# Seven block products for 22 of the 30 query, key and value blocks of each mixer, in a phase of their own

## The chip, the cores and the metric

One core of one Trainium2 chip. The metric is the device time of one execution in microseconds (us); lower is better.

## What is computed

Two layers of an encoder on 512 tokens of 1024 channels, all in float32. A layer is a feed-forward half-step, a mixer and a second feed-forward half-step. The change is in the mixer, which reads (cut):

```
u = rmsnorm(h, mix_pre_g[l])
proj = u @ w_in[l]
qa, ka, va, qb, kb, vb, qc, kc, vc, gl = jnp.split(proj, split_at, axis=-1)
oa = neighbourhood_attention(qa, ka, va, na_rpb[l])             # 8 heads
ob = sliding_window_attention(rope(qb), rope(kb), vb, sink[l])  # 8 query, 2 key heads
oc = differential_attention(rope(qc), rope(kc), vc, lam, ...)   # 4 heads, two maps each
yb = einsum('bsnc,ncd->bsnd', stack([oa, ob, oc], axis=2), w_branch[l])
gates = sigmoid(gl.reshape(b, s, 3, 1024) + b_gate[l])
h = h + rmsnorm(sum(gates * yb, axis=2) @ w_out[l], mix_post_g[l])
```

`w_in` has 54 column blocks of 128: four each of QA, KA, VA, QB, QC, KC and VC, one each of KB and VB (30 in all), and 24 of the gates (GL).

## The kernel before

Activations are kept transposed: channels on the 128 partitions, 512 tokens along the row. To keep float32 precision every operand is split into a rounded high part and a low part, and a product of two blocks is three matmuls, high by high, high by low, low by high (`mm3`, lines 319 to 324). A **plain dense block** (`dense1`, line 341) is one column block of a weight matrix: 8 row blocks, so 24 matmuls of 512 columns. A block against `w_branch` (`combine`, line 1584) has 4 row blocks, so 12 matmuls. Weights stream in tiles of 512 KB; ScalarE (ACT) makes the high part and VectorE (DVE) the low part of four blocks at a time (`ensure`, lines 220 and 221).

The feed-forwards (`ffn`, line 587) already take their gate and up blocks another way for most of the pairs: the activations and the weights are cut into 2 by 2 quarters, and **seven products** of quarters replace the eight of a plain pair (groups `p1` to `p7`, lines 892 to 913; the matmuls stand on line 878). A group of two column blocks is 7 x 4 x 3 = 84 matmuls of 256 columns. Sums of weight quarters and their splits are made by DVE and ACT for each group (lines 712 to 764), and quarter sums of the activations once for each feed-forward (lines 694 to 708).

In the mixer (`mixer`, line 1434) all 30 query, key and value blocks and the 24 gate blocks are plain. The first three (QA, KA, VA of pair 0) are made in the handover from the feed-forward (`begin`, line 402). Query and key blocks are evicted, rotated for branches B and C (`rope`, line 1421: four copies between partitions and three DVE operations), split, and copied into stacks with the high part over the low part (`stacks`, line 1336); value blocks are turned by TensorE transposes (`turn`, line 1352). A head of branches A and B is `softmax_pv` (line 1375): scores into a PSUM bank, DVE adds the bias and finds the maximum (line 1388), ACT takes the exponential (1397), DVE divides by the sum (1404), TensorE transposes (1412), the result is split, and two matmuls for each key block make the output (1415, 1416). Branch C is `attn_c` (line 1522). A gate block is evicted by ACT as a tanh (line 1581) and kept on the chip; `combine` multiplies it with the branch block on DVE (line 1588), and POOL adds it to the sum (line 1592).

The order of the work is the string `ORDER` (line 68), which traces units such as `qa1` (a pair's query, key and value blocks), `aa1` (its attention), `ga3` (a gate) and `ya3` (a branch block) one after the other. A compile-time scheduler then places the instructions of each engine by that order as a priority: what stands later may run ahead when its inputs and buffers are there. The ends of the phases are ordered by hand (`ordered`, line 416). PSUM has eight banks: four for dense blocks (`mm`), three for scores, transposes and small things (`at`), one for the head's output (`o`). Weight fetches of the mixer are issued on ACT's queue, those of the groups and nearly all other transfers on SP's.

## Time and profile before

| | before |
|---|---|
| median of 3 runs | 2397.39 us (2397.25 to 2400.49) |
| the profiled execution's span | 2398.4 us |
| TensorE (PE) busy | 2371.4 us, 99% |
| VectorE (DVE) busy | 1791.3 us, 75% |
| ScalarE (ACT) busy | 1340.1 us, 56% |
| GpSimd (POOL) busy | 155.3 us, 6% |
| moved by DMA | 340.45 MB, mean 142 GB/s |

The profiled execution's own time is its span, 2398.4 us from the first to the last instruction, 1.0 us above the median of the runs. Matmuls overlap in the profile (each is shown for longer than the distance to the next), so their pace is read from the distance between starts, or from evictions a known number of matmuls apart. The first mixer lies from about 347 to 858 us, the second from about 1547 to 2066 us; the rest are feed-forwards.

### The profile page before, as it was taken

Reading aid. Unit: us, or ns where it says so; the run is one execution under the profiler, and the core shown is the slowest. Engines: PE = TensorE matmul, PEld = TensorE weight load, DVE = VectorE, ACT = ScalarE, POOL = GpSimd, SP = SyncE. Lnnn points to the kernel's source line nnn. Section 1 sums busy time; section 2 is a strip of 40 time slices with the busy share of each in tenths; the row PEclk is TensorE's granted clock in tenths of the full one; section 3 lists DMA queues with packets and bytes.
Section 4 is the critical chain, followed back from the end, with each engine's and each line's share of the span. In section 5 each row is a group of like instructions: output and inputs, shape, how many; then the busy total and the mean of one; then the engine's idle time right before and its main releaser. Section 6 shows DMA issues by size and latency. Waiting matters only on the chain. (4 is left out here: it accounts for less than half of the span.)

```text
span 2398.4 us, 37669 instructions
## 1 busy us (share of the span) xinstructions
PE 2371.4 (99%) x14266; PEld 2083.0 (87%) x14266; DVE 1791.3 (75%) x2986; ACT 1340.1 (56%) x2493; POOL 155.3 (6%) x166
## 2 busy tenths in 40 slices
PE   9999999999999999999999999999999999999998
PEld 8999887888787889998899998878877788899987
DVE  7887975858767477888878878767676764788796
ACT  6565655646555365655655555556555554556563
POOL 0111000000001100110001110000000011011100
PEclk9999999999999999999999999999999999999999
DMA  5566546434443334665525565364354433346642
GB/s 168 160 172 188 162 142 177 128 106 138 123 135 97 106 111 136 164 165 166 174 90 166 160 176 192 120 186 121 104 142 129 110 104 123 97 144 172 185 147 91
DMA packets 119189, 340.45 MB, mean 142 GB/s; under 512 B 15968, under 2 KB 22752, under 8 KB 118496
## 3 DMA queue, kind: packets, MB, share of 16 engines
q1 hardware_dynamic: 91344, 224.72, 30.3%
q10 hardware_dynamic: 22032, 79.78, 11.1%
q0 software_dynamic: 5632, 33.56, 6.9%
q8 instruction: 112, 1.84, 0.3%
q14 instruction: 69, 0.57, 0.1%
HBM read 285.03 MB, written 48.23 MB: 139 GB/s over the span
## 5 line engine op out<-in xcount | busy, mean ns | idle before, releaser
L322 PE MATMUL mm<-X,w 128*128 128x512 f32 (+1 forms) x1044 | 396.5, 380 | 3.9 <-ACT w L220 2.1
L323 PE MATMUL mm<-X,w 128*128 128x512 f32 (+1 forms) x1044 | 396.7, 380 | 0.7 <-DVE X L550 0.7
L324 PE MATMUL mm<-X,w 128*128 128x512 f32 (+1 forms) x1044 | 395.0, 379 | 0.0
L221 DVE TENSOR_TENSOR w<-wr,w 128x512 fp32r<-128x512 f32 x360 | 250.3, 700 | 163.0 <-ACT w L220 161.5
L220 ACT ACTIVATE w<-wr 128x512 fp32r<-128x512 f32 x360 | 223.5, 627 | 222.7 <-PE mm L324 177.3
L878 PE MATMUL mm<-ht,l 128*128 128x256 f32 x1120 | 310.9, 278 | 0.0
L878 PE MATMUL mm<-ht,h 128*128 128x256 f32 x1120 | 310.9, 278 | 0.0
L878 PE MATMUL mm<-lt,h 128*128 128x256 f32 x1120 | 310.5, 277 | 0.0
L322 PEld LDWEIGHTS mm<-X,w 128*128 128x128 f32 x1044 | 197.2, 189 | 36.6 <-ACT X L549 2.6
L323 PEld LDWEIGHTS mm<-X,w 128*128 128x128 f32 x1044 | 197.3, 189 | 32.5 <-DVE X L550 1.1
L324 PEld LDWEIGHTS mm<-X,w 128*128 128x128 f32 x1044 | 197.1, 189 | 32.0
L878 PEld LDWEIGHTS mm<-lt,h 128*128 128x128 f32 x1120 | 210.8, 188 | 0.0
L878 PEld LDWEIGHTS mm<-ht,l 128*128 128x128 f32 x1120 | 210.6, 188 | 0.0
L878 PEld LDWEIGHTS mm<-ht,h 128*128 128x128 f32 x1120 | 210.5, 188 | 0.0
L1119 PE MATMUL mm<-wh,f 128*128 128x512 f32 x640 | 200.2, 391 | 0.0
L878 PE MATMUL mm<-X,h 128*128 128x256 f32 x1120 | 198.8, 277 | 0.0
L878 PEld LDWEIGHTS mm<-X,h 128*128 128x128 f32 x1120 | 170.0, 188 | 0.3
L878 PE MATMUL mm<-X,l 128*128 128x256 f32 x560 | 154.8, 277 | 0.0
L1119 PEld LDWEIGHTS mm<-wh,f 128*128 128x128 f32 x640 | 120.2, 188 | 25.5
L734 DVE TENSOR_TENSOR l<-wr,h 128x1024 fp32r<-128x1024 f32 x70 | 85.7, 1224 | 66.3 <-PE mm L878 66.3
L1119 PE MATMUL mm<-wl,f 128*128 128x512 f32 x320 | 125.5, 392 | 0.0
L1592 POOL TENSOR_TENSOR gate<-gate,gate 128x512 f32<-128x512 f32 x32 | 49.8, 1562 | 1155.3 <-DVE gate L1588 1049.3
(372 smaller groups left out, 5424.9 us busy)
## 6 DMA issues: line engine op xcount, KB each, us to landing
wr<-in_wts_dram SPq DMA_DIRECT2D x223, 512.0 KB, 4.7
wr<-in_wts_dram ACTq DMA_DIRECT2D x152, 512.0 KB, 3.6
sum<-in_wts_dram POOLq DMA_DIRECT2D x64, 512.0 KB, 5.4
st<-hi SPq DMA_DIRECT2D x84, 128.0 KB, 2.3
st<-lo SPq DMA_DIRECT2D x84, 128.0 KB, 3.7
ap<-in_wts_dram SPq DMA_DIRECT2D x20, 512.0 KB, 6.4
a<-kept SPq DMA_DIRECT2D x32, 256.0 KB, 6.3
ap<-sum SPq DMA_DIRECT2D x16, 512.0 KB, 3.3
```

The lines of the kernel that those rows point to most:

```text
L220: A.activation(hi, raw, AF.Copy)
L221: V.tensor_tensor(out=lo, in0=raw, in1=f(hi), op=ALU.subtract)
L322: PE.matmul(acc, w[0], x[0], start=start, stop=False)
L323: PE.matmul(acc, w[0], x[1], start=False, stop=False)
L324: PE.matmul(acc, w[1], x[0], start=False, stop=stop)
L734: V.tensor_tensor(out=W[g]["l1"], in0=raws[g][0], in1=f(W[g]["h1"]), op=ALU.subtract)
L878: PE.matmul(acc, ws[i], xs[j], start=start and k == n == 0, stop=stop and k == HK - 1 and n == 2, skip_group_check=True,)
L1119: PE.matmul(acc, x[i], w[j], start=start and n == 0, stop=stop and n == 2, skip_group_check=True)
L1592: G.tensor_tensor(out=merged[m], in0=merged[m], in1=t, op=ALU.add)
```

## The change

A new phase `p` (`project`) stands between the first feed-forward and the mixer of each layer. It makes all 30 blocks: eight of them plain (`COVER`, three in the handover as before) and 22 in 11 seven-product groups (`GROUPS`), with the feed-forward's group code moved into a class `Seven`. The first feed-forward's handover therefore also makes raw copies of its result, as the second's did. Query and key blocks of A, QB and KB are evicted, rotated where needed, split and written to memory; so are the turned and split values; QC and KC are written raw. Pair 0 of branch A stays on the chip. The mixer keeps attention, gates and branch blocks; it loads stacks and values from memory, and rotates and splits QC and KC after loading them. The second half of a head (transposes and output) is traced behind the scores of the next head (`rest`, `follow`). Scores have two banks of their own (`mx`), dense blocks two instead of four. Branch A's division by the sum moves from DVE to ACT. Gates of B and C are written to memory and loaded back for `combine`, through two tiles (`gd`). The order is new. The diff, cut to its core:

```diff
+COVER = (QA, KA, VA, QA + 1, KA + 1, VA + 1, KB, VB)
+GROUPS = (
+    (QA + 2, KA + 2), (VA + 2, VA + 3), (QA + 3, KA + 3), (QB, QB + 1), (QB + 2, QB + 3), (QC, KC), (QC + 1, KC + 1),
+    (VC, VC + 1), (QC + 2, KC + 2), (QC + 3, KC + 3), (VC + 2, VC + 3),
+) + tuple((GL + 2 * i, GL + 2 * i + 1) for i in range(0))
...
-qa0 qa1 aa0 aa1 qa3 qa2 aa3 aa2 kb ga2 ga1 ga0 qb0 ga4 ga5 ga7 ya5 ga3
-ga6 ab0 qb1 ya1 ya2 ya6 ya7 ab1 qb3 qb2 ya3 ya0 ya4 ab3 ab2 qc1 qc0 gb4
-gb0 gb1 ac0 yb0 yb1 qc2 gb2 yb2 ac1 gb3 qc3 gb5 ac2 yb4 yb5 gb6 yb6 fc2
-gb7 ac3 yb3 gc0 fc1 yb7 fc0 fc3 gc1 gc2 yc0 yc1 gc3 yc3 gc4 yc4 gc5 yc2
-gc7 gc6 yc6 yc7 yc5
+qa0 qa1 aa0 ga0 ga1 qa2 aa1 ga2 qa3 aa2 ga3 ga4 kb qb0 aa3 ga5 qb1 ab0
+ga6 ga7 gb0 qb2 ab1 gb1 gb2 qb3 ab2 ya0 gb3 ya1 gb4 qc0 ab3 ya2 gb5 ya3
+qc1 ac0 gb6 ya4 gb7 qc2 fc0 ac1 ya5 gc0 ya6 fc1 qc3 ac2 gc1 ya7 gc2 fc2
+ac3 yb0 gc3 yb1 gc4 fc3 yb2 gc5 yb3 gc6 yb4 gc7 yb5 yb6 yb7 yc0 yc1 yc2
+yc3 yc4 yc5 yc6 yc7
...
-    ABUFS = {"f": {"t": 4, "x": 10}, "m": {"t": 5, "h": 4, "rr": 2, "tx": 5, "st": 16, "g": 10, "s": 2, "pt": 4}}
-    PBUFS = {"mm": 4, "at": 3, "o": 1}
+    ABUFS = {"f": {"t": 4, "x": 10}, "p": {"t": 16, "x": 10, "rr": 2}, "m": {"t": 5, "h": 4, "rr": 2, "tx": 5, "st": 14, "gd": 2, "g": 10, "s": 2, "pt": 4}}
+    PBUFS = {"mm": 2, "mx": 2, "at": 3, "o": 1}
...
+        def seed_banks(self, x):
+            self.seeds = [bank("at") for _ in range(2)]
+            for t in self.seeds:
+                PE.matmul(t, x[:, 0, 0, :P], x[:, 0, 0:2, :], start=True, stop=True)
+
...
+    def project(l, op, accs):
...
+        def store(kind, x):
+            d = dr.tile([P, T], F32, tag=kind, name=nm(kind), bufs=60)
+            nc.sync.dma_start(d, f(x))
+            return d
...
+            made[c] = store("part", hi), store("part", lo)
...
+                made[c] = v if c == VA else [store("part", t) for t in v]
+            else:
+                made[c] = [store("part", t) for t in parts(tp)]
...
+        def turned_by(c, x):
+            sh = big("t", name="sh")
+            for q in range(4):
+                o = q ^ 1
+                nc.sync.dma_start(sh[32 * q : 32 * q + 32], x[32 * o : 32 * o + 32])
+            slowly.extend(
+                (
+                    lambda: V.tensor_tensor(out=x, in0=x, in1=turning[0], op=ALU.mult),
+                    lambda: V.tensor_tensor(out=sh, in0=sh, in1=turning[1], op=ALU.mult),
+                    lambda: V.tensor_tensor(out=x, in0=x, in1=sh, op=ALU.add),
+                    lambda: stacked(c, x),
+                )
+            )
...
+        def ready(c, x):
+            if c < VA:
+                stacked(c, x)
+            elif QB <= c < VB:
+                turned_by(c, x)
+            elif c < QB or c == VB:
+                turned(c, x, 2)
+            elif c >= VC:
+                turned(c, x, 1)
+            else:
+                made[c] = store("raw", x)
+
...
+        rest = [dense1(w, l, COVER[3], X, tag="at")]
+        for c, acc in zip(COVER, list(accs) + rest):
+            out(c, acc)
+        for n, c in enumerate(COVER[4:]):
+            out(c, dense1(w, l, c, X, tag=("mm", "at")[n % 2]))
+        while later:
+            later.pop(0)()
...
+        S.seed_banks(op.hi[0])
...
+                S.add22(g)
+            S.p2(g)
+            first_half(g)
+            if more:
+                S.low12(g + 1)
+                S.sum4(g + 1)
+                if g + 2 < count:
+                    S.fetches(g + 2)
+                else:
+                    fetch(1, nc.sync)
+                S.p5(g)
+                S.high24(g + 1)
+            work(3)
+        S.p3(count - 1)
+        second_half(count - 1)
+        other(count - 1)
+        work(len(slowly))
...
+            if sink is None:
+                A.activation(ss[i], ss[i], AF.Copy, scale=l[:, i : i + 1])
+            else:
+                V.tensor_scalar(out=ss[i], in0=ss[i], scalar1=l[:, i : i + 1], scalar2=None, op0=ALU.mult)
+        def rest():
+            op = bank("o")
...
+        def ask(hd):
+            raw = raws[hd] = big("g", name="braw")
+            nc.sync.dma_start(raw, bass.AP(rpb.tensor, (l * 8 + hd) * 16 * RPBW, [[RPBW, 8], [1, 16], [1, 8 * RPBW]]))
...
+        def load(d, dt=F32, tag="tx"):
+            x = big(tag, dt, name="x")
...
+        def rope(c):
+            x = load(made[c])
+            sh = big("tx", name="sh")
+            for q in range(4):
+                o = q ^ 1
+                nc.sync.dma_start(sh[32 * q : 32 * q + 32], made[c][32 * o : 32 * o + 32])
...
+            for s in range(2):
+                own, pair_ = slice(64 * s, 64 * s + 64), []
+                for one, two in ((hi, lo), (lo, hi))[: 2 if both else 1]:
+                    st = big("st", F32R, name="st")
+                    nc.sync.dma_start(f(st)[0:64], one[own])
+                    nc.sync.dma_start(f(st)[64:128], two[own])
+                    pair_.append(st)
+                res.append((pair_ + [None])[:2])
...
+        def follow(rest):
+            settle()
+            pending.append(rest)
...
+        def qkv_a(p):
+            for s in range(2):
+                ask(2 * p + s)
+            return restacked(QA + p, False), restacked(KA + p, True), values(VA + p)
...
+                rest = softmax_pv(
...
+                follow(rest)
...
-                t = gate0[m // 4][:, m % 4, :] if n == 0 else big("g", name="gate")
+                t = gate0[m // 4][:, m % 4, :] if n == 0 else big("gd", name="gate")
                 A.activation(t, pg, AF.Tanh, scale=0.5, bias=col("b_gate", l, n * KD + m))
+                if n:
+                    d = dr.tile([P, T], F32, tag="gate", name=nm("gate"), bufs=4 * KD)
+                    nc.sync.dma_start(d, t)
+                    t = d
                 gate[n, m] = t
...
+                if n:
+                    t = load(t, tag="gd")
...
+        with open_phase("p"):
+            made = project(l, X, accs)
         with open_phase("m"):
-            X, accs = mixer(l, X, accs)
```

## Rows read from the trace of the kernel before

**Rows 1.** The page: span, and busy us of each engine with its share, x instructions.

```profile
span 2398.4 us, 37669 instructions
...
PE 2371.4 (99%) x14266; PEld 2083.0 (87%) x14266; DVE 1791.3 (75%) x2986; ACT 1340.1 (56%) x2493; POOL 155.3 (6%) x166
```

**Rows 2.** Busy time by stretch; (x) instructions; last three: granted clock, DMA share, GB/s.

```profile
131.41:217.31 85.90, 85.90 (x754) 85.90 (x753) 72.66 (x92) 50.16 (x84) 14.97 (x18) 1.00 0.62 164
334.00:347.00 13.00, 12.61 (x64) 10.37 (x63) 11.45 (x20) 7.78 (x19) 0.00 (x0) 1.00 0.23 80
347.00:707.00 360.00, 354.48 (x1820) 294.54 (x1819) 248.46 (x610) 197.89 (x464) 4.30 (x3) 1.00 0.48 133
707.00:780.00 73.00, 72.60 (x352) 57.67 (x351) 52.12 (x104) 41.66 (x80) 10.32 (x7) 1.00 0.36 108
870.00:905.00 35.00, 35.00 (x230) 32.24 (x231) 24.74 (x35) 21.35 (x36) 0.00 (x0) 1.00 0.21 67
1190.00:1210.00 20.00, 20.00 (x125) 17.96 (x126) 16.57 (x31) 13.81 (x34) 0.00 (x0) 1.00 0.23 79
```

**Rows 3.** TensorE's waits: who waited for whom, us in all, times, longest.

```profile
PE at L1412 <- DVE s L1404: 2.9, 4, 1.9
```

**Rows 4.** Line 917, seed copy, once per group; 131 to 218 us; ns min/median/max, starts.

```profile
L917 ACT ACTIVATE at<-mm x10: 360/367/368, 131.4 to 217.3; 128x256 f32<-128x256 f32 x10
```

**Rows 5.** Timeline of ACT, 484 to 512 us: start, us, gate evictions [idle before].

```profile
490.86 0.69 ACT L1581 ACTIVATE gate<-mm,colt 128x512 f32<-128x512 f32 x1 [1.10 <-PE mm L324]
...
496.30 0.69 ACT L1581 ACTIVATE gate<-mm,colt 128x512 f32<-128x512 f32 x1 [2.09 <-PE mm L324]
```

**Rows 6.** PE's weight loads, 131 to 217 us: busy us, mean ns.

```profile
L878 PEld LDWEIGHTS mm<-ht,h 128*128 128x128 f32 x143 | 26.9, 188 | 0.0
```

**Rows 7.** DVE, 131 to 217 us: the gating product of the feed-forward.

```profile
L946 DVE TENSOR_TENSOR a<-t,v 128x512 f32<-128x512 f32 x9 | 6.1, 682 | 0.0
```

**Rows 8.** DVE by line and form, 347 to 780 us: count, busy us, mean ns.

```profile
L221 DVE TENSOR_TENSOR w<-wr,w 128x512 fp32r<-128x512 f32 x113 | 79.6, 705 | 48.4 <-ACT w L220 48.2
...
L1404 DVE TENSOR_SCALAR s<-s,l 128x256 f32<-128x256 f32 x48 | 14.7, 349 | 0.4
L349 DVE TENSOR_TENSOR lo<-x,hi 128x512 fp32r<-128x512 f32 x21 | 14.4, 688 | 6.4 <-ACT hi L348 4.8 <-DMA st<-hi 1.2
L349 DVE TENSOR_TENSOR lo<-at,hi 128x512 fp32r<-128x512 f32 x20 | 13.6, 687 | 7.6 <-ACT hi L348 7.6
...
L1429 DVE TENSOR_TENSOR x<-mm,cosR 128x512 f32<-128x512 f32 x13 | 8.9, 686 | 1.7 <-DMA sw<-lo 1.0 <-ACT raw L1423 0.7
...
L1362 DVE TENSOR_TENSOR v<-at,v 128x256 fp32r<-128x256 f32 x10 | 4.2, 420 | 1.7 <-ACT v L1361 1.7
```

**Rows 9.** Timeline of ACT, 380 to 480 us: head outputs (L1418), gates (L1581).

```profile
408.34 0.60 ACT L1418 ACTIVATE ot<-o 64x512 f32<-64x512 f32 x1
...
456.03 0.70 ACT L1581 ACTIVATE gate<-mm,colt 128x512 f32<-128x512 f32 x1
...
477.79 0.60 ACT L1418 ACTIVATE ot<-o 64x512 f32<-64x512 f32 x1
```

**Rows 10.** DMA issues: queue, count, KB each, median us from issue to landing.

```profile
wr<-in_wts_dram ACTq DMA_DIRECT2D x152, 512.0 KB, 3.6
...
a<-kept SPq DMA_DIRECT2D x32, 256.0 KB, 6.3
...
mask<-in_tables_dram SPq DMA_DIRECT2D x2, 256.0 KB, 4.5
```

**Rows 11.** The gates' combination on DVE and POOL, whole span.

```profile
L1592 POOL TENSOR_TENSOR gate<-gate,gate 128x512 f32<-128x512 f32 x32 | 49.8, 1562 | 1155.3 <-DVE gate L1588 1049.3 <-DVE nm L1536 80.4 <-DVE lc L1544 25.5
...
L1588 DVE SCALAR_TENSOR_TENSOR gate<-gate,mm 128x512 f32<-128x512 f32 x48 | 32.9, 685 | 25.0 <-PE mm L324 24.4
```

More of the change, by code (lines that the diff above doesn't have):

```diff
@@ L916, in seed @@
[L916 to L932 removed]
+        S.seed_banks(X.hi[0])
@@ L1442, in mixer @@
+        return rest
+    def mixer(l, op, made):
+        w, X = "w_in", op.blocks
+        masks, raws, turning = {}, {}, []
         for c0, n in ((0, 512), (512, 256)):
@@ L1577, in gates @@
+            follow(rest)
+        gate, merged = {}, [None] * KD
+        gate0 = made["gates"]
+        while len(gate0) < 2:
+            gate0.append(sb.tile([P, 4, T], F32, tag="n", name=nm("gate"), bufs=BUFS["n"]))
+        for _, c in GROUPS:
+            for m in (c - 1 - GL, c - GL) if c > GL else ():
+                gate[0, m] = gate0[m // 4][:, m % 4, :]
         def gates(n, *ms):
@@ L1614, in do @@
             kind, i = u[:2], int(u[2:] or 0)
+            if kind == "fc" or kind[0] == "y":
+                if kind == "fc" and i >= len(oc) or kind[0] == "y" and (kind[1], 3) not in OT:
+                    settle()
             if kind == "qa":
-                if i == 0:
-                    held[u] = qkv_a(*first)
-                else:
-                    early = second if i == 1 else []
-                    late = [dense1(w, l, c + i, X) for c in (QA, KA, VA)[len(early) :]]
-                    held[u] = qkv_a(*early, *late)
+                held[u] = qkv_a(i)
             elif kind == "kb":
-                held["kb"] = qkv_b(KB), turn(plain(dense1(w, l, VB, X), False), 2)
+                tables_in()
+                held["kb"] = qkv_b(KB), values(VB)
             elif kind == "qb":
@@ L1642, in mixer @@
             do(u)
-        M = [split(merged[m], "st", 0.5) for m in range(KD)]
+        M = [split(merged[m], "st" if m < 7 else "gd", 0.5) for m in range(KD)]
         hN = [big("s", shape=(P, 2, 2, T), name="h") for _ in range(2)]
```

682 lines of the change are left out of this document (427 added, 255 removed).

## The prediction, made before the result was known

> **What bounds the kernel now.** I read the page first: TensorE is busy for 2371.4 of the 2398.4 us of the span, VectorE (DVE) for 75% of it [rows 1]. So a matmul taken away is worth its full time as long as nothing else becomes late, and an engine at 75% is the one to watch. Then the table of stages, for idle time by stage: TensorE has none at all in the seven-product groups of a feed-forward (131 to 217 us), and 5.9 us (433 less 354.48 and 72.60) in the mixer from 347 to 780 us; the granted clock is 1.00 in each of these, the 2.4 GHz level [rows 2]. Then TensorE's list of waits, for what ends that idle time: the largest entry is a transpose that waits 2.9 us in all for a scaled score block from DVE [rows 3]. What is to be seen: the mixer is bound by TensorE because dense blocks fill the waits inside the attention. The change takes 27 of those fillers out of the mixer.
>
> **The change, part by part.** The sum is made on the profiled execution (2398.4 us, 1.0 us above the median of the runs).
>
> *Seven products.* Ten groups of a feed-forward lie nine periods apart, from 131.41 to 217.31 us: 9.54 us for one group of 84 half-width matmuls [rows 2, 4]. A pair of plain blocks is 48 full-width matmuls; two gate evictions with nothing between them lie 5.44 us apart [rows 5], so a pair takes 10.88 us. One group saves 1.34 us; 11 groups in each of 2 layers save 29.5 us.
>
> A half-width matmul carries a weight load of its own, of 188 ns [rows 6], and the rows show that it is hidden: 9.54 us over 84 is 114 ns a matmul, half of the 227 ns of 5.44 us over 24. The Trainium skill (TensorE: Matmul & The Clock Gate, Back-to-back issue gap) gives a sustained spacing of about 81 ns at 128 columns and 131 ns at 512 for streams of load and matmul; a straight line between them puts 256 columns at 98 ns (an estimate from that page), by which a group would cost 8.2 us against 6.3 us for a pair, and the change would lose 42 us. The trace disagrees with both of its spacings here.
>
> *Seeds.* Two more full-width matmuls in each layer (`seed_banks`), 4 x 0.227 = 0.9 us, on the path.
>
> *DVE in the new phase.* A group of the feed-forward costs DVE 72.66 / 9 = 8.07 us; without the gating product of 0.68 us it is 7.4 us [rows 2, 7]. The new phase adds the blocks' own work: rotating a block is three operations of 0.69 us and its split one more (2.75 us; five blocks), splitting a Q or K block of branch A 0.69 us (four), two value blocks of A 0.84 us each, four of C 0.69 us each [rows 8]: 20.9 us over 11 groups, 1.9 us each. That makes 9.3 us of DVE work against 9.54 us of TensorE. The cover is only 0.2 us a group, and the highest DVE share of a stretch in which TensorE did not wait is 85% (72.66 of 85.9) [rows 2]. Bounds: nothing, or 9.3 / 0.85 = 10.9 us a group, 15 us a layer. I take 1 us a layer, near the lower end, because weights are prepared a whole group ahead and the rotations are dealt out three at a time. ScalarE (50.16 of 85.9 us there) has room.
>
> *Ahead of the groups.* The eight plain blocks of this phase have the cover of the feed-forward's 870 to 905 us, where TensorE never waits and DVE has 10 us free [rows 2]; their evictions add about 3 us of DVE work: nothing. The raw copies that the first feed-forward's handover now makes are made today by the second's, where TensorE is busy 20.00 of 20 us, as against 12.61 of 13 in the first's [rows 2]: nothing, and if ScalarE were late there, 0.4 us.
>
> *Attention with less cover.* From 347 to 780 us TensorE loses 27 blocks of 5.44 us (three of the 30 were in the handover): 433 - 147 = 286 us remain. DVE has 248.46 + 52.12 = 300.6 us there [rows 2]; off go 54 weight splits of 0.705 us, 13 block splits of 0.69, five rotations of 2.06, ten value splits of 0.42 and four of 0.69, and the scaling of branch A's 32 score blocks of 0.35 that goes to ScalarE: 75 us [rows 8]. So 225 us over 286, 79% after 69%. But the new order ends on five gates and 16 branch blocks behind the last head, which need little DVE: 5 x 5.44 + 16 x 2.73 (12 matmuls of 0.227) = 71 us of TensorE with 26 splits and 16 combinations, 29 us of DVE. Ahead of them stand 215 us of TensorE against 196 us of DVE, 91%. At the 85% above those 196 us last 231: 16 us longer than TensorE's work. Two things speak for less. The program's order is run ahead of where it can be: gates that stand behind branch A's last two pairs were evicted from 456.03 us on, before its last head left at 477.79 [rows 9]; 49 us of the tail (five gates, eight blocks of branch B) can be run ahead the same way. And heads now overlap, where branch A's leave one by one, seven steps in 69.45 us [rows 9]. Bounds per layer: 5.9 us gained (all idle time gone) to 16 us lost. I take 5 us lost: cover gets thinner in the same stage that already waits.
>
> *From one phase to the next.* Masks and bias tables are loaded into tiles that lie where the new phase's were; a mask lands 4.5 us after its issue [rows 10]. Behind it wait the first head's scores; the first gates (5.44 us each, weights ready) cover it. Bounds 0 to 5 us a layer; I take 0.5.
>
> *Gates through memory.* Gates of branches B and C are written out and come back into a ring of two tiles (`gd`), on SP's queue. Stores wait in that queue for the tanh, loads for POOL's addition, and the stack loads and bias loads behind them wait with them; those are asked for a pair ahead. At the end 11 branch blocks follow each other. One turn of a tile is the load, 0.69 us on DVE and 1.56 us on POOL [rows 11]. Nearest rows for the load: 3.6 us (weights, twice the size) and 6.3 us (a kept row of this size, in a burst) [rows 10]. That gives (3.6 + 2.25) / 2 = 2.9 us a block against 2.73, or 4.3 us: 2 to 17 us a layer for 11 blocks. I take 2, since only one load is asked for at a time there, as with the weights.
>
> *Banks and transfers.* A dense block now has two banks in place of four; one is needed again 5.44 us (2.73 for a branch block) after its last matmul, and its eviction takes 0.69 us [rows 5, 11]: nothing, as long as that engine is less than 2 us late. In each layer 46 blocks of 256 KB are stored, twelve MB in about 105 us, on SP's queue between the weight fetches; they wait for splits that stand a few us ahead of the next fetch, and the sums that fill this stretch's queues in a feed-forward (0.62 of the DMA engines) are absent [rows 2]: nothing, and up to 0.5 us a group if a fetch does get caught behind a store, which is within the bound given for DVE there. Later the same halves are loaded as are copied on the chip today, plus 16 values and 16 gates.
>
> *Sum.* -29.5 + 0.9 + 2 x (1 + 5 + 0.5 + 2) = -11.6 us on 2397.4: **2386 us**.
>
> **Rivals.**
> 1. *All of it hidden* (2369 us). The overlap of heads and the run-ahead cover everything: -29.5 + 0.9. With today's idle time gone too it would be 2357. For it: seven-product groups already run without a wait at 85% of DVE. Against it: 91% ahead of the tail.
> 2. *DVE paces the attention* (2408 us, slower). Place: from the first head to the last of branch C. Price: 16 us a layer in place of my 5, so 2386 + 22. It decides from the point at which the scheduler runs less than 11 us of the tail's blocks ahead. If DVE also paced the new phase (15 us a layer) it would be 2436. Against it: today's order does run ahead [rows 9].
> 3. *The gate ring paces the tail* (2416 us). Place: the 11 branch blocks at the end; price 17 us a layer in place of 2. It decides once a gate takes over 3.2 us to land (2 x 2.73 less 2.25). For it: 6.3 us for the kept rows; against it: those are eight at once.
> 4. *Seven products cost more, not less*: half-width matmuls held to their 188 ns weight load would make a group 15.8 us, 4.9 above a pair, 108 us slower (2505 us). The groups of [rows 4] exclude it where they are; the page named above would have it in kind.
>
> **How the numbers follow.** My forecast has a chance of 0.46, rival 1 0.19, rival 2 0.25, rival 3 0.09, rival 4 0.01. The forecast's own range is 2376 to 2397. A measurement of this kernel can tell about 0.2% from no change, 4.8 us: faster is below 2392.6, slower above 2402.2. Faster: nearly four fifths of my forecast (0.36) and rival 1, 0.55. Same: the upper end of the forecast and the mild parts of rivals 2 and 3, 0.15. Slower: the rest, 0.30. The range, 2363 to 2416, takes in rival 1 with half of today's idle time gone below, and rivals 2 and 3 at their prices above; what is left out is both at once, or the new phase paced by DVE.
>
> **What would show it.** Right: groups of 9.5 to 9.7 us in the new phase; TensorE idle there under 3 us a layer; in the mixer between 8 and 14 us idle with DVE at 78 to 85%, waits ended by DVE; combinations in the tail 2.8 to 3.0 us apart. Wrong: periods over 10 us with DVE full (DVE paces the new phase); a mixer idle of 25 us or more (rival 2); combinations over 4 us apart that wait for a load (rival 3); no idle time at all (rival 1). What would make me wrong without showing in these: a transfer on SP's queue that holds the stacks of the next pair back, seen as scores waiting for a DMA.

## The result: 2405.4 us, 0.24% slower; the range held, the sign did not

| | before | after |
|---|---|---|
| median, same chip | 2399.62 us (9 runs, 2394.58 to 2402.60) | 2405.37 us (9 runs, 2398.53 to 2408.37) |
| ratio, 95% interval | | 1.0024 [1.0013, 1.0035] |
| the profiled execution's span | 2398.4 us | 2403.6 us |

The page of the changed kernel, the lines that answer to [rows 1]: TensorE's busy time fell by 14.6 us, with 796 more matmuls, and the span grew by 5.2.

```profile
span 2403.6 us, 39852 instructions
...
PE 2356.8 (98%) x15062; PEld 2109.1 (88%) x15062; DVE 1891.1 (79%) x3048; ACT 1425.7 (59%) x2671; POOL 156.5 (7%) x166
```

Busy time is not the whole of it, since a matmul at the lower clock counts as busy. So I split both spans another way: each matmul at its usual spacing (227 ns for 512 columns, 113.5 for 256, the same in both kernels), TensorE's idle time in the mixers (counted from the new phase's start), and what the granted clock took away, which is (1 less the granted clock) times the time that TensorE was busy at it.

| us, both layers | before | after | difference | forecast |
|---|---|---|---|---|
| matmuls at their usual spacing | 2325.3 | 2296.2 | -29.1 | -28.6 |
| idle time in the mixers | 14.3 | 33.8 | +19.5 | +17 |
| lost to the lower clock there | 0 | 9.0 | +9.0 | no term |
| the rest | 58.8 | 64.6 | +5.8 | no term |
| span | 2398.4 | 2403.6 | +5.2 | -11.6 |

The first row is a count times fixed spacings, as the forecast's was, so it shows only that the count was right; the pace itself is read from the groups below. The idle time as a sum came near the forecast. What turned the sign is the two rows under it: the lower clock follows waits, and the rest is what this account does not place. The clock differs from run to run: of the nine runs of the changed kernel the fastest, 2398.53 us, has a mean granted clock of 0.997, the others 0.994 to 0.996. Here are the stages of the first mixer in the changed kernel, in the columns of [rows 2]: cover blocks, seven-product groups, the start of the attention, its middle, branch C, the tail.

```profile
335.30:398.00 62.70, 62.36 (x371) 54.98 (x369) 48.23 (x71) 39.18 (x78) 0.00 (x0) 1.00 0.45 140
398.00:508.00 110.00, 109.26 (x942) 108.12 (x941) 91.80 (x126) 70.41 (x132) 0.00 (x0) 1.00 0.61 201
508.00:560.00 52.00, 46.05 (x238) 38.06 (x237) 28.93 (x97) 34.77 (x95) 0.00 (x0) 0.97 0.81 208
560.00:700.00 140.00, 139.06 (x737) 116.14 (x736) 123.60 (x336) 102.76 (x263) 0.00 (x0) 1.00 0.59 173
700.00:760.00 60.00, 57.66 (x267) 45.61 (x266) 48.18 (x100) 32.69 (x67) 5.01 (x3) 0.97 0.72 209
760.00:860.00 100.00, 94.97 (x429) 75.41 (x429) 57.89 (x100) 45.59 (x86) 20.48 (x13) 1.00 0.48 150
...
530.00:533.00 3.00, 3.00 (x12) 2.51 (x12) 0.00 (x0) 0.00 (x0) 0.00 (x0) 0.56 0.86 252
...
718.00:721.00 3.00, 3.00 (x11) 2.41 (x10) 2.55 (x6) 1.15 (x3) 0.00 (x0) 0.52 0.07 25
...
1715.80:1718.50 2.70, 2.66 (x16) 2.37 (x17) 0.42 (x1) 0.45 (x3) 0.00 (x0) 1.00 0.69 208
...
1733.60:1736.00 2.40, 2.40 (x8) 1.91 (x8) 0.00 (x0) 0.00 (x0) 0.00 (x0) 0.50 0.69 202
...
1906.70:1909.00 2.30, 2.30 (x6) 1.82 (x7) 1.98 (x4) 0.60 (x1) 0.00 (x0) 0.50 0.04 13
```

Three of the six stages lose time, and not the one in the middle, where DVE is busy for 88%: start 5.95 us, branch C 2.3, tail 5.0 (in the second layer 7.8, 3.3 and 5.4). The short windows stand behind long waits. Behind four of them, of 3.80, 1.90, 4.65 and 2.88 us, TensorE comes back at 0.50 to 0.56, that is, at the 1.2 GHz level for all or most of the window, and is busy all the while, with few matmuls done (6 in 2.3 us at 1906.7). Behind four others the clock stays at 1.00: 2.69 us (the window from 1715.8), and 1.65, 1.67 and 2.04 us (at 546, 798 and 1989 us). So the length of a wait alone does not decide it here.

TensorE's list of waits in the changed kernel names the three causes (us in all, times, longest):

```profile
PE mx L1659 <- DMA st<-part: 12.8, 4, 4.7
PE mm L326 <- DVE x L1912: 8.2, 8, 2.0
PE o L1871 <- DVE lo L353: 4.8, 2, 2.9
```

**Start.** The scores of branch A's pair 1 wait for stacks. The timeline of SP's queue there, and in branch C (start, us, line, DMAs):

```profile
516.37 0.80 SPq L1762 DMA_DIRECT2D st<-part  x1
...
520.54 0.45 SPq L1762 DMA_DIRECT2D st<-part  x1
526.09 0.45 SPq L1763 DMA_DIRECT2D st<-part  x1
...
707.84 1.02 SPq L465 DMA_DIRECT2D gain<-in_rows_dram  x2
708.95 0.58 SPq L1739 DMA_DIRECT2D x<-raw  x1
...
712.22 1.79 SPq L465 DMA_DIRECT2D gain<-in_rows_dram  x2
```

Masks and bias tables go first, the first stack is asked for at 516.37 us, and the queue then stops for 5.5 us behind the issue at 520.54, and again later. The queue's own list of waits (505 to 545 us) says what ended the two long stops:

```profile
SPq L1763 <- DMA wr<-in_wts_dram: 11.0, 2, 5.9
```

That is no transfer of this queue, but a weight load, issued on ACT's queue (for the first stop at 516.77 us, landed at 526.07). The program gives its transfers eight semaphores in turn, over both queues; the stack's load takes over the weight load's, and is not issued before that has landed. No run here gives the two their own semaphores, so how much of the wait this makes is open. Over the start the DMA engines are busy for 0.81 at 208 GB/s.

**Branch C.** The handover's gain rows, 1 MB and not needed for another 140 us, are issued around a query block's loads. DVE's timeline shows what that does: the rotation (L1748) waits 2.91 us for its load, and the split that TensorE needs (L353) stands behind it on the same engine. The second fence has TensorE's rows, the first of them for the start, the second for branch C.

```profile
715.08 0.69 DVE L1748 TENSOR_TENSOR x<-x,cosR 128x512 f32<-128x512 f32 x1 [2.91 <-DMA x<-raw]
716.35 1.28 DVE L353 TENSOR_TENSOR lo<-at,hi 128x512 fp32r<-128x512 f32 x2
```

```profile
529.94 0.47 PE L1659 MATMUL mx<-st,st 128*128 128x256 f32 x2 [3.80 <-DMA st<-part]
...
717.09 0.50 PE L1871 MATMUL o<-lo,x 128*128 128x512 f32 x1 [1.90 <-DVE lo L353]
```

**Tail.** Combinations (L1912) come 3.74 us apart where a branch block takes 2.73. The timelines of DVE, POOL and ACT, interleaved by start here, show a closed loop from the second row on: combination, POOL's addition, the high part on ACT, the low part on DVE, and only then the next combination. DVE's queue holds the low part ahead of that combination. The tail's longest wait (1.67 us at 798 us, 2.04 in the second layer) is not of this loop: there the combination itself waits for a gate's load, as the first row shows. That load was issued at 793.68 us, when POOL's addition had just freed one of the two tiles.

```profile
797.44 0.69 DVE L1912 SCALAR_TENSOR_TENSOR x<-x,mm 128x512 f32<-128x512 f32 x1 [1.74 <-DMA x<-gate]
...
812.22 0.68 DVE L1912 SCALAR_TENSOR_TENSOR x<-x,mm 128x512 f32<-128x512 f32 x1
813.04 1.61 POOL L1916 TENSOR_TENSOR gate<-gate,x 128x512 f32<-128x512 f32 x1 [2.13 <-DVE x L1912]
814.68 0.63 ACT L355 ACTIVATE hi<-gate 128x512 fp32r<-128x512 f32 x1 [2.59 <-POOL gate L1916]
815.35 0.69 DVE L356 SCALAR_TENSOR_TENSOR lo<-gate,hi 128x512 fp32r<-128x512 f32 x1 [1.85 <-ACT hi L355]
815.96 0.68 DVE L1912 SCALAR_TENSOR_TENSOR x<-x,mm 128x512 f32<-128x512 f32 x1
```

**Groups.** The seed copies of the new phase, once per group, in the columns of [rows 4]: ten periods in 98.9 us, 9.89 us each (10.08 in the second layer).

```profile
L719 ACT ACTIVATE at<-mm x11: 363/369/392, 398.5 to 497.4; 128x256 f32<-128x256 f32 x11
```

### The profile page after: what moved, and what is told of

Same layout as the page of the kernel before. It is cut to its first block, busy times and chain, and to the rows that moved or that the text cites. A ratio compares the mean times of both kernels' runs of the same rounds, so it can differ in the third digit from the quotient of the medians.

```text
span 2403.6 us, 39852 instructions
## 1 busy us (share of the span) xinstructions
PE 2356.8 (98%) x15062; PEld 2109.1 (88%) x15062; DVE 1891.1 (79%) x3048; ACT 1425.7 (59%) x2671; POOL 156.5 (7%) x166
## 5 line engine op out<-in xcount | busy, mean ns | idle before, releaser
L326 PE MATMUL mm<-X,w 128*128 128x512 f32 (+1 forms) x602 | 229.6, 381 | 3.1 <-ACT X L553 1.8
L327 PE MATMUL mm<-X,w 128*128 128x512 f32 (+1 forms) x602 | 229.1, 380 | 0.8 <-DVE X L554 0.7
L328 PE MATMUL mm<-X,w 128*128 128x512 f32 (+1 forms) x602 | 229.6, 381 | 0.0
L680 PE MATMUL mm<-ht,l 128*128 128x256 f32 x736 | 205.8, 280 | 0.0
L680 PE MATMUL mm<-ht,h 128*128 128x256 f32 x736 | 205.6, 279 | 0.0
L680 PE MATMUL mm<-lt,h 128*128 128x256 f32 x736 | 204.9, 278 | 0.0
L680 PE MATMUL mx<-lt,h 128*128 128x256 f32 x736 | 203.6, 277 | 0.0
L680 PE MATMUL mx<-ht,h 128*128 128x256 f32 x736 | 203.5, 277 | 0.0
L680 PE MATMUL mx<-ht,l 128*128 128x256 f32 x736 | 203.4, 276 | 0.0
L680 PE MATMUL at<-X,w 128*128 128x256 f32 x1104 | 141.2, 277 | 0.0
L680 PEld LDWEIGHTS mx<-lt,h 128*128 128x128 f32 x736 | 138.3, 188 | 0.1
L680 PEld LDWEIGHTS mx<-ht,h 128*128 128x128 f32 x736 | 138.2, 188 | 0.1
```

Of the source, the lines that this page charges most:

```text
L326: PE.matmul(acc, w[0], x[0], start=start, stop=False)
L327: PE.matmul(acc, w[0], x[1], start=False, stop=False)
L328: PE.matmul(acc, w[1], x[0], start=False, stop=stop)
L680: PE.matmul(acc, ws[i], xs[j], start=start and k == m == 0, stop=stop and k == n - 1 and m == 2, skip_group_check=True,)
```

## The experiments

Each ratio is to the kernel before, run on the same chip. What an edit does to the changed kernel is the difference of its ratio from 1.0024, times 2400 us, good to some 4 us. Diffs are against the changed kernel unless the text says otherwise.

### Two of the three waits mended

**e2, the gain rows later.** Their loads are issued behind those of branch C's first gate.

```diff
-        H = Handover(
+        with tc.issue_after(behind[0].ins):
+            H = Handover(
```

> Edit: the four row loads of the handover's gains (L465) are issued behind the first gate load of branch C on SP's queue, no longer beside the load of the last key block of branch C. Theory (that key block lands late because 1 MB of gains is loaded beside it, VectorE's rotation waits 2.9 and 3.9 us for it, and TensorE's second matmul of a C output waits behind that): the stalls of 1.90 us at 717.1 and 2.88 us at 1906.6 us go, and the half clock behind them, so the time falls by 7 to 10 us (4.8 us of waiting and about 5 us of half clock). Rival (the block is late because of its own stacks and weights in that stretch, the gains make no difference): the stalls stay within 1 us of what they are and the time within 3 us.

Measured: 2396.99 us, 0.9990 [0.9980, 1.0001], 8 us better than the changed kernel. The list of waits and the windows around branch C of both layers:

```profile
PE mx L1659 <- DMA st<-part: 11.8, 3, 4.4
PE mm L326 <- DVE x L1914: 7.3, 9, 1.2
```

```profile
700.00:740.00 40.00, 38.42 (x178) 29.77 (x177) 29.95 (x62) 22.01 (x44) 1.79 (x1) 1.00 0.68 181
1890.00:1920.00 30.00, 29.42 (x141) 22.78 (x139) 23.96 (x49) 14.55 (x29) 0.00 (x0) 1.00 0.75 206
```

L1871 falls from 4.8 to 0.5 us and the clock stays at 1.00. The two waits showed 4.8 us of idle time and gave 8 back. That points to a wait that costs more than its length, but 4.8 lies within the 4 us to which the 8 is known.

**e3, each split of the tail behind the next combination.** It takes the loop apart and leaves the ring of two gates as it is, so it tells the loop from rival 3's gate loads.

```diff
-        M = [split(merged[m], "st" if m < 7 else "gd", 0.5) for m in range(KD)]
+        M = []
+        for m in range(KD):
+            with tc.issue_after(made_[2, min(m + 1, KD - 1)].ins):
+                M.append(split(merged[m], "st" if m < 7 else "gd", 0.5))
```

> Edit: in the tail VectorE's split of merged block m is queued behind combination m+1, not ahead of it; the ring of two gate tiles stays. Theory (a loop over four instructions: combination, POOL's addition, ScalarE's high part, VectorE's low part, and the next combination stands behind that low part in VectorE's queue): combinations come down from 3.74 to 2.7 to 3.0 us apart, TensorE's waits of 0.74 us for them go, and the time falls by 5 to 9 us in the two layers. Rival (the ring of two gate tiles sets the 3.74 us: load, combination, addition): they stay over 3.5 us apart and the time within 2 us.

Measured: 2400.61 us, 1.0002 [0.9990, 1.0014], 5 us better. DVE's timeline in the tail:

```profile
811.13 0.67 DVE L1913 SCALAR_TENSOR_TENSOR x<-x,mm 128x512 f32<-128x512 f32 x1
...
814.19 0.68 DVE L1913 SCALAR_TENSOR_TENSOR x<-x,mm 128x512 f32<-128x512 f32 x1
```

3.06 us apart in place of 3.74, and TensorE's waits of 0.74 us are gone. The loop was the cause of the 3.74. The ring of two gates has another part: the first wait of the tail stays (1.88 and 1.96 us), and in this run too the combination ahead of it waits for a gate's load (1.95 us at 799.86).

**e6, both.** The edits of e2 and e3 together.

```diff
+        with tc.issue_after(behind[0].ins):
...
+            with tc.issue_after(made_[2, min(m + 1, KD - 1)].ins):
```

> Edit: e2 and e3 together (gains late, splits behind the next combination). Theory (each loss stands by itself in its own stage): the gains add up, 8.4 and 4.8 us, to 2391 to 2395 us. Rival (what is won in one stage is lost in the next): less than the better of the two, 2396 us or more.

Measured: 2394.36 us, 0.9977 [0.9967, 0.9987]. It beats both kernels: 11 us off the changed one, near the sum of the two (13.5). What stands at the head of its list is the start, with 14.9 us; no other entry is over 3.0:

```profile
PE mx L1659 <- DMA st<-part: 14.9, 4, 5.1
```

### The wait at the start, which no edit could turn into time

**e1, gates ahead of the scores.** The scores of pair 1 are held behind gate 3, those of pair 2 behind gate 5.

```diff
-qa0 qa1 aa0 ga0 ga1 qa2 aa1 ga2 qa3 aa2 ga3 ga4 kb qb0 aa3 ga5 qb1 ab0
+qa0 qa1 aa0 ga0 ga1 qa2 ga2 ga3 aa1 qa3 ga4 ga5 aa2 kb qb0 aa3 ga6 qb1 ab0
...
+BEHIND = {1: (0, 3), 2: (0, 5)}
...
+            with tc.issue_after(behind.ins) if behind else ExitStack():
```

> Edit: four gates of branch A stand ahead of pair 1's scores on TensorE (two gates and three quarters before), six ahead of pair 2's. Theory (the stacks that come back from memory land after TensorE asks for them, and each such stall of several us also costs the clock): the stalls of 3.80 and 1.65 us at 529.9 and 546.3 us and of 2.69 and 4.65 us at 1715.8 and 1733.6 us go, the granted clock in 530 to 536 and 1733 to 1740 us is 1.00, and the time falls by 10 to 17 us (12.8 us of waiting and about 5 us of half clock, less what thinner cover later gives back). Rival (VectorE paces the attention as a whole): idle time only moves to the stretch from 560 to 760 us, time within 4 us of the changed kernel's.

Measured: 2415.11 us, 1.0067 [1.0053, 1.0081], 10 us worse. Pair 1 no longer waits for its stacks, but a later head does wait (4.75 us at 557), and waits ended by DVE and ACT follow; idle time in the mixers is 47 us after 33.8. The theory fell. Of the rival, idle time did move on, but the kernel is 10 us slower and not within 4.

**e5, wider rows.** A pair's stacks in 6 transfers with rows of 4 KB in place of 14 with 2 KB; the two kinds of limit, number of issues and bytes, come apart.

```diff
+            if not both:
+                st = twin()
+                nc.sync.dma_start(f(st), d)
+                return [(st[:, s, :], None) for s in range(2)]
...
+                for n in range(2):
+                    nc.sync.dma_start(f(st)[64 * n : 64 * n + 64], d[own, n : n + 2, :])
```

> Edit: the blocks are written out in the form in which they are needed, so that a pair's queries come back in one transfer, its keys in four and its values in one, 6 in place of 14, in rows of 4 KB in place of 2 KB; bytes read are the same, bytes written are more by one key part a block. Theory (at the start of the mixer the stacks are late because of the many small rows and issues, not because of the order on TensorE, which e1 changed without gain): the stalls for stacks at the start of each mixer (5.5 and 7.3 us) fall below 2 us a layer, the half clock behind them (5 us lost in all) goes, and the time falls by 10 to 17 us, to 2388 to 2395 us. Rival (the bytes or the memory's answer set it, not the rows): the stalls stay within 2 us of what they are, the time within 4 us.

Measured: 2428.88 us, 1.0124 [1.0108, 1.0140], 24 us worse. Over the same 52 us of the start the DMA engines (last but one column) are as busy as before, 0.82 after 0.81, and move no more, 200 GB/s after 208:

```profile
508.00:560.00 52.00, 43.05 (x231) 35.85 (x230) 26.92 (x91) 31.92 (x87) 0.00 (x0) 0.93 0.82 200
```

So fewer issues and longer rows did not make the loads faster. The edit changes more than that, though: it also stores a third part for each key block, and the stacks come in fewer and coarser transfers. The waits for stacks were 16.3 us in all.

**e7, e5 with the two mends.** The edits of e2, e3 and e5 together.

```diff
+        with tc.issue_after(behind[0].ins):
...
+                st = twin()
```

> Edit: e2, e3 and e5 together. Theory (late transfers at the start and in branch C, the loop in the tail, and the clock behind them are all that stands between the changed kernel and its 29 us): 2374 to 2384 us, faster than the kernel before by 0.7 to 1.0 per cent, with under 12 us of idle time in both mixers together beyond what the kernel before has there (14.3 us). Rival (VectorE is the next limit and gives the time back in the attention): over 2388 us with new waits that VectorE ends between 560 and 760 us.

Measured: 2425.79 us, 1.0121 [1.0102, 1.0140]. Missed as e5 was: the two mends, worth 11 us on the changed kernel, are worth 1 on top of e5.

**e9, fewer bytes: pair 1's queries and values stay on the chip,** in the tile of the raw copies.

```diff
-            if c in (QA, KA):
+            if c in (QA, KA, QA + 1):
...
-                made[c] = v if c == VA else [store("part", t) for t in v]
+                made[c] = v if on is not None else [store("part", t) for t in v]
```

> Edit: the queries' stacks and the values of branch A's pair 1 stay on the chip, in the tile whose raw copy is done with early in the new phase (1 MB less to read back a layer, and as much less to write). Theory as it stands after e1 and e5 (the start of the mixer is bound by the DMA engines, busy for 0.9 to 1.0 of the time between 520 and 540 us at some 220 GB/s; what counts is how many bytes must land before pair 1, some 4.4 MB from 511 to 530 us): 1 MB at 220 GB/s is 4.6 us earlier for pair 1 and for what follows it, so the stalls of 3.80 and 2.69 us for pair 1 go, those for pair 2 (1.65 and 4.65 us) fall to under 2 us, the half clock there (5 us lost) mostly goes, and the time falls by 8 to 16 us. Rival (the place on SP's queue or the number of issues sets it): the stalls for stacks at the start stay above 8 us in the two layers together, the time within 4 us.

Measured: 2416.27 us, 1.0069 [1.0056, 1.0082], 11 us worse. The load side did what was expected: pair 1's scores start at 526.5 us, 3.4 earlier for 1 MB less. But the list now has the middle of the attention on it:

```profile
PE mx L1662 <- DMA st<-part: 6.0, 4, 2.8
PE o L1696 <- DVE l L1678: 5.5, 2, 2.9
```

**e10, e9 with the two mends.**

```diff
+            if c in (QA, KA, QA + 1):
...
+        with tc.issue_after(behind[0].ins):
```

> Edit: e9 with e6 (gains late, splits behind the next combination). Theory (the three places are independent): 2394 less 8 to 16 us, 2378 to 2387 us, faster than the kernel before by 0.5 to 0.9 per cent. Rival (VectorE takes over as the limit of the attention): over 2390 us.

Measured: 2409.81 us, 1.0042 [1.0028, 1.0056], 15 us worse than e6. Missed as e9 was; the two mends gave 6 us on top of e9.

**e11, still fewer bytes.** This kernel leaves out reading the low parts of branch A's keys and values from memory: one key stack and one value part are loaded for a pair and used twice. All instructions of the engines stay.

```diff
-                for one, two in ((hi, lo), (lo, hi))[: 2 if both else 1]:
+                for one, two in ((hi, lo), (lo, hi))[: 2 if both and c >= QB else 1]:
...
-                res.append((pair_ + [None])[:2])
+                res.append((pair_ * 2 if both else pair_ + [None])[:2])
```

> Edit: for branch A's pairs 1 to 3 only one of the two key stacks of a head and only one of the two value parts are read back, and used twice (the kernel leaves out reading the low parts there; matmuls, VectorE, ScalarE and order stay): 1.25 in place of 2 MB a pair. Theory (the start of the mixer is bound by the bytes that must land, and nothing else follows behind it): the stalls for stacks and values from 520 to 620 us fall from 5.5 us to under 2 us a layer, the granted clock there is 1.00, and the time falls by 9 to 17 us against the changed kernel. Rival (relieving the start uses up the dense blocks sooner and the time is lost later in the attention, as e9 seemed to show): less than 4 us, with new stalls of over 2 us between 560 and 760 us.

Measured: 2418.98 us, 1.0083 [1.0068, 1.0098], 14 us worse. The waits for stacks fell from 12.8 to 5.5 us, and others took their place, one of them ended by ACT, which is busy 19.82 of the 20 us ahead of it (fourth busy column):

```profile
PE o L1693 <- ACT hi L352: 5.9, 2, 3.0
PE mx L1659 <- DMA st<-part: 5.5, 3, 2.6
```

```profile
540.00:560.00 20.00, 19.36 (x113) 15.77 (x112) 18.48 (x60) 19.82 (x58) 0.00 (x0) 1.00 0.81 235
```

With e9 this shows that the loads end that wait but do not set the end: what comes earlier there is lost again later. In e11 as in e9 the stretch from 560 to 700 us has over 5 us of idle time (134.62 and 133.89 busy of 140), where the changed kernel has 0.9.

### The engines in the middle

**e4, branch A's scaling back on DVE.** It puts rival 2's question: has DVE room in the attention?

```diff
-                A.activation(ss[i], ss[i], AF.Copy, scale=l[:, i : i + 1])
+                V.tensor_scalar(out=ss[i], in0=ss[i], scalar1=l[:, i : i + 1], scalar2=None, op0=ALU.mult)
```

> Edit: one part of the change undone, the scaling of branch A's score blocks goes back from ScalarE to VectorE (32 operations of some 0.35 us a layer, 11 us). Rival (VectorE paces the attention): the time rises by most of 2 x 11, 15 to 22 us. Theory (TensorE is full in the middle of the attention with VectorE at 75 to 97 per cent, and what is lost is lost to late loads and in the tail): it rises by less than 6 us.

Measured: 2419.46 us, 1.0079 [1.0062, 1.0095], 13 us worse, between the two expectations. 64 operations of 0.35 us, 11 us a layer, made this wait, between 561 and 640 us and at the same place in the second layer:

```profile
PE o L1694 <- DVE lo L353: 11.6, 6, 3.6
```

So DVE does not fully pace the changed kernel (13 us for 22 us of added work), but there is little room: 11 us of 140 is less than a tenth.

**e15, half of it on DVE, with the two mends,** to share the load between the two engines.

```diff
+                if i % 2:
+                    V.tensor_scalar(out=ss[i], in0=ss[i], scalar1=l[:, i : i + 1], scalar2=None, op0=ALU.mult)
+                else:
+                    A.activation(ss[i], ss[i], AF.Copy, scale=l[:, i : i + 1])
```

> Edit: e6, and the scaling of branch A's score blocks divided, every second one on VectorE and the others on ScalarE. Theory after e11 (under the late loads at the start lies a full ScalarE, 19.8 of 20 us busy from 540 to 560 us in e11): a few us faster than e6 where it is ScalarE that paces, 2388 to 2394 us. Rival (VectorE has less room than ScalarE over the whole attention, as e4 showed with 13 us for twice the move): 3 to 8 us slower than e6.

Measured: 2408.68 us (ten runs from 2400.0 to 2413.5), 1.0039 [1.0026, 1.0052], 15 us worse than e6 and outside both expectations. Idle time in the middle went from 1.4 us in e6 to 5.6 (140 less 138.57 and 134.35).

**e8, heads one by one.** The overlap of heads undone.

```diff
-            pending.append(rest)
+            rest()
```

> Edit: one part of the change undone: the second half of a head (transposes, output, addition) is traced right behind its first half again, not behind the next head's scores. Theory (the overlap covers VectorE's and ScalarE's chain within a head, and with 22 blocks fewer as cover it is needed): 8 to 25 us slower than the changed kernel, with TensorE waiting for transposes between 560 and 760 us. Rival (the compile-time scheduler runs later heads ahead by itself): within 4 us.

Measured: 2408.05 us, 1.0040 [1.0028, 1.0053], 4 us worse, which is no more than the 4 us to which it is known. The rival's number held: the overlap that the change writes out is worth little. That the scheduler runs ahead by itself is the likely reason; no row here shows it.

### What a wait costs beyond its length

Three kernels that are the kernel **before** with waits put into the groups of its feed-forwards, where TensorE has no idle time. A small matmul waits, and the group's next product is held behind it.

**e13, 24 short waits** (for a copy on ACT).

```diff
+            held_up.append(PE.matmul(bank("o")[:16, :16], src[:, :16], src[:, :16], start=True, stop=True))
...
+            with tc.issue_after(held_up[-1].ins) if held_up else ExitStack():
...
+            if g in PLACES:
+                hold_up(g)
```

> Edit, to the kernel before: the same wait without the transfers, so that TensorE waits only for ScalarE's copy (some 0.8 us), in six groups of each feed-forward, 24 times in all. Theory (short waits cost their length): about 19 us of idle time, the time rises by that within 2 us, and the granted clock stays at 1.00. Rival (any idle time costs clock as well): it rises by 1.3 to 1.7 times the idle time that the profile shows.

Measured: 2423.81 us, 1.0106 [1.0088, 1.0123]. TensorE's timeline, one wait and the next:

```profile
96.38 0.21 PE L883 MATMUL o<-v 128*16 128x16 f32 x2 [0.47 <-ACT v L936]
...
106.88 0.21 PE L883 MATMUL o<-v 128*16 128x16 f32 x2 [0.47 <-ACT v L936]
```

A group took 10.50 us in place of 9.54 [rows 4]: 0.96 for a wait that shows 0.47 (0.91 when each group is set against the same group of the kernel before). The other half microsecond the profile shows as busy; I put it down to draining and refilling, but 0.14 of it is the small matmul itself (the next product starts at 96.52). 24 of them are 23 us, and 25 were measured. The granted clock stayed at 1.00 behind all 24. Neither expectation held: no clock was lost, and yet a wait cost twice its length.

**e12, four long waits** (two transfers of 8 KB behind each other), with a small tile of their own.

```diff
+            for _ in range(HOPS):
+                dst = small("stall", 16, 2)
+                nc.sync.dma_start(dst, src[:, :16])
```

> Edit, to the kernel before: in one seven-product group of each feed-forward TensorE waits for a value that two transfers of 1 KB have to carry first, some 5 us, four times in all; nothing else changes. The groups there run at full clock without a wait. Theory (a stall of several us costs its length and, behind it, a stretch of TensorE at 1.2 GHz): 20 us of idle time and 7 to 14 us more, so the time rises by 27 to 34 us, and the granted clock behind each stall is 0.50 for 3 to 7 us. Rival (a stall costs its own length): it rises by the idle time within 2 us, and the clock stays at 1.00.

Measured: 2463.11 us, 1.0267 [1.0252, 1.0283], 64 us, far too much for four waits. A stretch of groups without any wait explains it, first the kernel before, then e12:

```profile
140.00:220.00 80.00, 80.00 (x703) 80.00 (x702) 66.53 (x85) 46.30 (x77) 13.18 (x16) 1.00 0.62 168
```

```profile
140.00:220.00 80.00, 80.00 (x680) 80.00 (x679) 66.13 (x84) 45.30 (x74) 13.17 (x16) 1.00 0.58 160
```

118 ns a matmul after 114, in all four feed-forwards. The likely cause is that the new tile of 128 bytes moved all tiles behind it. So this run says nothing of waits.

**e14, the same in room that was already there.**

```diff
+                dst = room[:, 12 * n : 12 * n + 12]
+                nc.sync.dma_start(dst, src[:, :12])
```

> Edit: e12 again, with the two small tiles of the wait laid into 96 bytes that the kernel already sets aside and does not use, so that no other tile moves (in e12 every later tile moved by 128 bytes, and all its seven-product matmuls ran at 118 ns in place of 114, far from the stalls too). Theory (a long stall costs its length and a stretch at 1.2 GHz behind it): matmuls at 114 ns again away from the stalls, four stalls of 5 to 8 us, granted clock 0.50 behind each, and the time rises by the four stalls' own length plus 6 to 10 us. Rival (the length alone): by the stalls' length within 2 us. What e12 had beyond both, some 25 us, was the moved tiles and goes.

Measured: 2435.71 us, 1.0149 [1.0136, 1.0162]; the matmuls are back at 114 ns (701 in those 80 us). TensorE's timeline at the first wait, and the windows ahead of it and behind it:

```profile
121.64 0.22 PE L883 MATMUL o<-room 128*12 128x12 f32 x2 [7.14 <-DMA room<-room]
```

```profile
112.00:114.30 2.30, 2.30 (x23) 2.30 (x21) 1.17 (x2) 0.65 (x2) 0.00 (x0) 1.00 0.04 18
121.60:124.00 2.40, 2.36 (x12) 2.32 (x13) 0.00 (x0) 0.00 (x0) 0.00 (x0) 0.50 0.03 7
124.00:126.00 2.00, 2.00 (x11) 2.00 (x11) 0.79 (x2) 1.06 (x1) 0.00 (x0) 0.50 0.00 0
126.00:128.00 2.00, 2.00 (x17) 2.00 (x16) 0.90 (x2) 0.90 (x2) 0.00 (x0) 0.88 0.05 16
```

The four waits are 7.14, 6.04, 6.40 and 6.47 us, 26.1 in all, and the kernel is 35.8 us slower: 10 us beyond their length. The clock took 2.4 us behind the first wait (1.2 + 1.0 + 0.2), and 2.4, 2.6 and 3.1 behind the others by the same sum, 10.5 in all; a refill as in e13 is not to be told apart beside it. The theory's 6 to 10 beyond the length held; a wait at its length alone is out.

## Why the prediction was wrong

Point by point.

*The seven products: right.* The matmuls that the forecast counted are the ones that ran, and their pace in the new phase is about 115 ns where 114 was forecast (9.89 us less 0.24 for the moved transposes, over 84). The spacings in the Trainium skill (TensorE: Matmul & The Clock Gate, Back-to-back issue gap) were again not this kernel's, and rival 4 is out. So is rival 1: not all of it was hidden.

*DVE in the new phase: right in idle time, a little short in the period.* Idle 1.1 and 1.7 us a layer, 1 taken. Periods of 9.89 and 10.08 us lie above the 9.5 to 9.7 that I gave: about 0.24 us of a group are the value transposes, which moved into this phase from the mixer and which I left out of its period. DVE is at 83% (91.80 of 110) and paces nothing.

*Attention with less cover: wrong in place.* I took 5 us a layer lost in the middle and got 0.9 and 0.3, at 88% of DVE; rival 2 did not occur. e4 and e15 show how near it lay.

*From one phase to the next: wrong in size.* I took 0.5 us of 0 to 5, because gates cover the masks. The masks were covered. What comes behind them on the queue was not: pair 1's stacks, two of whose issues waited until a weight load of the other queue had landed. With 6.0 and 7.8 us this term lies above its upper bound. The sentence that closed the prediction, of a transfer on SP's queue seen as scores that wait for a DMA, named the place and gave it no price.

*Gates through memory: too small, and half the mechanism missing.* TensorE waits 3.9 and 4.3 us for combinations after 2 (the rest of the tail's 5.0 and 5.4 are waits inside branch C's last heads), with combinations 3.74 us apart: between the forecast's 2.8 to 3.0 and rival 3's 4. In the steady stretch the load of the gate has no part in it. I priced one turn of a tile and not the order on DVE's queue, where the low part of one sum stands ahead of the next combination (e3). The turn of a tile, rival 3's mechanism, shows once a layer, in the tail's first wait of 1.67 and 2.04 us.

*Banks and transfers: wrong in one place.* I put transfers at nothing, going by what stands in SP's queue in a feed-forward, and left out what the handover puts there: 1 MB of gain rows ahead of branch C's loads, with DVE's rotation waiting and the split behind it (e2). 2.3 and 3.3 us.

*The step that failed* is the one that all these share: in the sum "2 x (1 + 5 + 0.5 + 2)" a microsecond of idle time costs a microsecond. The idle time itself came to 19.5 after 17, and that was luck: one term was too high and three were too low. It cost 34.3 in all: on top of it came 9.0 us of lower clock behind four waits of 1.9 to 4.65 us, and 5.8 us that the account does not place, in which the half microsecond that e13 shows behind each wait would lie. In the stages that I priced, TensorE has little idle time before the change (5.9 of the 433 us from 347 to 780) and a clock of 1.00 [rows 2], so no row there showed this price. The trace before has it elsewhere, though, in the first microseconds of the span, and it has a wait of much the same length in the second mixer behind which the clock stays up. TensorE's timeline for the first wait, then the windows behind both (the second wait, 1.92 us, ends at 1797.39):

```profile
10.68 0.39 PE L322 MATMUL mm<-X,w 128*128 128x256 f32 x1 [1.72 <-ACT w L220]
```

```profile
11.00:14.40 3.40, 3.40 (x18) 3.40 (x17) 2.73 (x6) 2.50 (x7) 0.00 (x0) 0.50 0.89 311
...
1797.40:1800.00 2.60, 2.60 (x16) 2.13 (x17) 2.26 (x6) 1.91 (x5) 0.00 (x0) 1.00 0.58 208
```

The Trainium skill had the price in kind too (TensorE: Matmul & The Clock Gate, HAM oscillation: a wait between bursts sends the array back to its lower clock, so that the loop pays for the wait and for the slow start behind it). The runs agree in part, with 0.50 behind waits of 1.9 to 7.1 us, but 1.00 behind others of 1.65 to 2.69 us, and behind all of 0.47.

*The chances.* With the 14.8 us that came on top of the idle time, the forecast's own idle time would have come to 2386 + 15 = 2401, no change. e6 shows what the change is worth without two avoidable waits: 0.23% faster.

*What stays open.* How much of the start's wait is the semaphore that stacks share with weight loads. Why an earlier start of pair 1 is lost again between 560 and 720 us; in e9 it is not the clock, since TensorE stands at 0.50 for 20.5 us in the mixers there as in the changed kernel. Every edit that changed what the scheduler sees in the attention (e1, e4, e5, e8, e9, e11, e15) cost 4 to 24 us (e15 against e6; e8's 4 are within the noise), also those that took work away. That the compile-time order suits just one set of arrival times, or that ACT is full there as in e11, are both possible; no run tells them apart.

## What to carry to other kernels

Price a wait of TensorE, in a stage that has none so far, at its length plus up to half a microsecond, and be ready for 1.7 to 3.1 us more behind a longer one, where the lower clock stays on behind it (here behind four of the eight waits of 1.65 us and more in the changed kernel, and behind all four of e14); several waits of 2 to 5 us can eat a saving that is there in full. When work moves through memory, follow each queue past the moved step and name what is issued on it that nobody needs yet and what else its issues wait for, and on each in-order engine name what stands behind an operation that waits for a load. Both mends here were a few lines each.

## What the hardware showed that I had not expected

- The granted clock reads 0.52 behind a wait of 1.9 us (718 to 721 us) and 0.50 behind one of 2.9 (1906.7), but 1.00 behind waits of 2.04 and 2.69 us in the same execution, and behind 24 waits of 0.47 us and the tail's 0.74.
- A wait of 0.47 us costs 0.96, with the small matmul that waits: the difference is shown as busy time.
- With one more tile of 128 bytes, 256-column matmuls took 118 ns in place of 114, and the whole kernel 28 us longer (1.0267 less 1.0149, of 2400); e12 and e14 differ in nothing else but the size of the small transfers. That the place of the tiles is the cause is likely, and not tested further.
- The DMA engines moved 208 GB/s over the start with rows of 2 KB (0.81 busy) and 200 with rows of 4 KB (0.82). A weight load of 512 KB, 3.6 us in the median before [rows 10], took 9.3 us there (516.77 to 526.07).
